# A hybrid attention and HGRN2 layer: the next input block prepared in mid-turn in the first head, eight shared buffers, half the descriptor area

## The chip, the cores and the metric

The kernel runs on one core of a Trainium2 chip. The metric is device time in microseconds (us), lower is better. TensorE is called PE, VectorE DVE, ScalarE ACT, GpSimd POOL and SyncE SP, as in the profile.

## What is computed

One layer over a sequence of 2048 rows of width 1024, all in float32:

```python
h = rmsnorm(x, ln1_w); proj = h @ w_in                 # 1024 -> 3584 columns
# four heads of differential attention (blocks of 128 queries, chunk-causal mask)
p = softmax(mask(q k^T / 8));  a = p[0] - lam * p[1];  o = rmsnorm(a @ v)
# four heads of HGRN2: a gated linear recurrence in chunks of 64 rows, with a carried state
x = x + concat(o_diff, o_hgrn) @ w_out
# feed-forward: up projection, causal convolution of width 3, SiLU gate, down projection
x = x + (silu(conv(u)) * v) @ w_down
```

## The kernel before

The program has four stages: the mixer (0 to about 1200 us), the output projection, the up projection and the down projection. The change is in the mixer, and one setting of it acts on the down projection too.

The mixer runs four heads one after the other (`s` = 0 to 3). A head does one attention head and one HGRN2 head over eight blocks of 256 rows (`b` = 0 to 7, called turns here). Each turn runs steps named by letters, in the order of a string:

```python
for b in range(NB):
    for c_ in ORDER if s else O0:
        nb_ = b + 1 + (c_ == "g" and s < GA) if c_ in "gABtuIJC" else b
        if nb_ < NB:
            step[c_](nb_)
```

The letters are: `g` makes or loads the normalized, transposed input block `hT`; `A`, `B` project q, k, v of the two halves of a block (24 matmuls of 384 columns each, L258 to L260); `I`, `J` project the value and gate of HGRN2 (24 matmuls of 256 columns each); `C` projects its query and forget gate (48 matmuls, tile `pjc`); `t`, `u` normalize and transpose q and k (tile `tpq`) and store `qT`; `a`, `b` are scores, maximum and exponentials of the two query blocks of a turn (tiles `sc`, `nm`, `p`); `x`, `y` blend the two softmaxes, transpose the blend and multiply with v (tiles `tpa`, `aT`, `av`); `h` is the level-by-level HGRN2 product (tiles `lt`, `kp`), `k` its output and state (tiles `op`, `sp`, `st`). `A`, `B`, `t`, `u`, `I`, `J`, `C` work on block b + 1, one turn ahead. In the first head `g` is one further ahead: in turn b it prepares block b + 2, so turns 0 to 5 hold it and turns 6 and 7 don't.

In the first head `g` is `phase1`: it loads two tiles `xt` of 128 rows (L225), squares and sums each on ACT (L233), takes the root on POOL (L103, L105), scales into `ht` on DVE (L235), transposes 16 blocks on PE into four PSUM tiles `tpx` (L241), evicts each in two halves by ACT (L244) and DVE (L245) into `hT`, and stores `hT` to DRAM (L247). In heads 1 to 3 `g` only loads `hT` back.

The order in which instructions reach each engine comes from the tile framework's list scheduler: the earlier an instruction stands in the program, the higher its priority; an instruction of lower priority goes ahead of one that isn't ready by the scheduler's own estimate. Engines then run their queues in order.

Buffers matter here. One pool, `pb`, with the tag `"p"` and `PBB` buffers of 4 KB a partition, holds the `xt` and `ht` of `phase1` (four of them for one block), the exponentials `p` of `a`, `b`, `x` and `y` (two for one query block in turns 0 to 3, four in turns 4 to 7, where the keys take two segments), and half of the first weight loads. In PSUM, `pj`, `pjc`, `tpq` and `tpx` share one tag with two buffers (`PJB`), and the scores `sc` have one (`SCB`).

The down projection keeps its sums in DRAM by 48 accumulating transfers that POOL issues (L830, `x2d<-acc`). Their descriptors are written by POOL into the area whose size `dynamic_dma_scratch_size` sets; all other transfers are issued by SP.

Of the kernel before, what the change touches and what calls it, by code (L numbers as in the profile page):

```python
# [67 lines left out]
def hymba_kernel(ctx, tc, x, ln1_w, w_in, q_norm_w, k_norm_w, lam_q1, lam_k1, lam_q2, lam_k2,  # L68
# [119 lines left out]
    with ExitStack() as ms:  # L188
# [73 lines left out]
        for s in range(4):  # L262
# [263 lines left out]
# [3 lines that stand above are left out]
# [353 lines left out]


ORDER = "gaABIbthJuxCyk"
O0 = "aABIbthJuxCgyk"
OF = "A1B23ItJuCg"
GA = 1
RB, QTB, FB, IGB, ATB, KVB, PBB = 4, 3, 2, 4, 3, 5, 6
SCB, PJB, MB = 1, 2, 2
AVT, AVB = "av", 1  # L890
HT, HB = "h", 1
# [35 lines left out]
```

## Time and profile before

| what | value |
|---|---|
| median of 3 runs | 2755.39 us (2753.69 to 2761.97) |
| the profiled execution, its own time | 2755.53 us |
| span of its trace | 2753.7 us |
| mean granted TensorE clock | 0.990 |
| PE busy / PEld (weight loads) busy | 2641.4 us (96%) / 2298.5 us (83%) |
| DVE, ACT, POOL busy | 1897.0 (69%), 1263.0 (46%), 1051.1 (38%) |

The span is the time from the first to the last instruction. A busy PE is a modelled figure: matmuls are pipelined, and one that starts while the one before still drains counts once.

### The profile page before, as it was taken

The numbers are of one execution on the slowest core, as the hardware profiler recorded it, in microseconds if no ns is written. First come the engines' busy times: TensorE is split into PE (matmuls) and PEld (weight loads), VectorE is DVE, ScalarE is ACT, GpSimd is POOL, SyncE is SP. The second block draws the span as 40 slices with busy tenths as digits, with TensorE's granted clock in tenths as the row PEclk, the third lists the DMA queues.
The fourth block names the chain that finished last, engine by engine and source line by source line (L and its number), as shares of the span: only waits on it lengthen the run. The fifth ranks groups of instructions, "written<-read, shape, count | busy, mean of one in ns | idle before, by whom it ended". The sixth has DMA issues, their size and how long they took to land. (4 is left out here: it accounts for less than half of the span.)

```text
span 2753.7 us, 42698 instructions
## 1 busy us (share of the span) xinstructions
PE 2641.4 (96%) x14722; PEld 2298.5 (83%) x14722; DVE 1897.0 (69%) x4058; ACT 1263.0 (46%) x3095; POOL 1051.1 (38%) x1168
## 2 busy tenths in 40 slices
PE   7999999999999999989999999999999998899999
PEld 6888999989999999978877888887888886687887
DVE  4677856676667666782337666668777769978787
ACT  4555644464446545553434434345434434334332
POOL 3222222212222222221234343443344346877775
PEclk9999999999999999999999999999999999999999
DMA  5333422232222322125754232235222224775754
GB/s 184 116 112 104 141 86 87 82 126 87 94 85 76 116 91 84 51 95 178 255 179 139 77 92 78 84 100 168 82 80 92 70 92 130 170 159 134 172 173 171
DMA packets 273492, 322.92 MB, mean 117 GB/s; under 512 B 19470, under 2 KB 238974, under 8 KB 269182
## 3 DMA queue, kind: packets, MB, share of 16 engines
q1 hardware_dynamic: 266366, 295.04, 32.7%
q0 software_dynamic: 6912, 25.17, 5.4%
q8 instruction: 117, 1.92, 0.3%
q14 instruction: 97, 0.79, 0.1%
HBM read 198.50 MB, written 104.86 MB: 110 GB/s over the span
## 5 line engine op out<-in xcount | busy, mean ns | idle before, releaser
L698 PE MATMUL q<-xT,WS 128*128 128x512 f32 x704 | 275.1, 391 | 2.3 <-DVE xT L631 2.2
L697 PE MATMUL q<-xT,WS 128*128 128x512 f32 x704 | 274.8, 390 | 2.3 <-ACT xT L630 2.3
L699 PE MATMUL q<-xT,WS 128*128 128x512 f32 x704 | 274.7, 390 | 0.0
L811 PE MATMUL pd<-TW,SG 128*128 128x512 f32 x616 | 245.0, 398 | 19.6 <-DVE acc L817 7.0
L813 PE MATMUL pd<-TW,SG 128*128 128x512 f32 x616 | 243.0, 396 | 3.3 <-DVE SG L631 3.3
L812 PE MATMUL pd<-TW,SG 128*128 128x512 f32 x616 | 244.0, 396 | 0.9 <-DVE TW L631 0.6
L630 ACT CAST WS<-st 128x512 fp32r<-128x512 f32 x176 | 108.5, 618 | 245.3 <-PE q L699 230.3
L698 PE MATMUL q<-xB,WS 128*128 128x512 f32 x528 | 207.1, 392 | 1.8 <-DVE xB L631 1.8
L697 PE MATMUL q<-xB,WS 128*128 128x512 f32 x528 | 207.3, 393 | 1.3 <-ACT xB L630 1.2
L699 PE MATMUL q<-xB,WS 128*128 128x512 f32 x528 | 206.9, 392 | 0.9 <-DVE WS L631 0.9
L387 ACT ACTIVATE p<-sc,nm 128x1024 f32<-128x1024 f32 (+4 forms) x192 | 165.5, 862 | 73.1 <-DVE nm L376 71.8
L631 POOL TENSOR_TENSOR WS<-st,WS 128x512 fp32r<-128x512 f32 x44 | 88.5, 2011 | 281.8 <-ACT WS L630 268.1
L376 DVE TENSOR_REDUCE nm<-sc 128x1 f32<-128x1024 f32 (+4 forms) x192 | 174.0, 906 | 12.6 <-PE sc L369 10.7
L258 PE MATMUL pj<-WA,hT 128*128 128x384 f32 x512 | 177.6, 347 | 2.6 <-DVE hT L245 2.6
L260 PE MATMUL pj<-WA,hT 128*128 128x384 f32 x512 | 175.4, 343 | 0.0
L259 PE MATMUL pj<-WA,hT 128*128 128x384 f32 x512 | 175.2, 342 | 0.0
L811 PEld LDWEIGHTS pd<-TW,SG 128*128 128x128 f32 x616 | 117.7, 191 | 49.9 <-DVE acc L817 8.3
L698 PEld LDWEIGHTS q<-xT,WS 128*128 128x128 f32 x704 | 132.5, 188 | 31.0 <-DVE xT L631 3.6
L697 PEld LDWEIGHTS q<-xT,WS 128*128 128x128 f32 x704 | 132.5, 188 | 30.0 <-ACT xT L630 2.8
L630 ACT CAST WS<-rawu 128x512 fp32r<-128x512 f32 x132 | 82.2, 624 | 163.4 <-PE q L699 163.0
L425 PE MATMUL av<-vst,aT 128*128 128x128 f32 x1088 | 151.0, 281 | 5.0 <-ACT aT L422 4.6
L699 PEld LDWEIGHTS q<-xT,WS 128*128 128x128 f32 x704 | 132.5, 188 | 27.4
(415 smaller groups left out, 7881.2 us busy)
## 6 DMA issues: line engine op xcount, KB each, us to landing
hT<-hTd SPq DMA_DIRECT2D x24, 2048.0 KB, 7.7
rawu<-in_w_up_dram SPq DMA_DIRECT2D x176, 256.0 KB, 3.0
x2d<-acc POOLq DMA_DIRECT2D x48, 512.0 KB, 6.4
gd<-c SPq DMA_DIRECT2D x176, 128.0 KB, 1.9
G<-gd SPq DMA_DIRECT2D x24, 768.0 KB, 4.4
hTd<-hT SPq DMA_DIRECT2D x8, 2048.0 KB, 6.2
qT<-qh SPq DMA_DIRECT2D x256, 64.0 KB, 2.0
rawd<-in_w_down_dram SPq DMA_DIRECT2D x22, 512.0 KB, 4.4
```

The lines of the kernel that those rows point to most:

```text
L258: PE.matmul(dst, lhsT=lh, rhs=rh, start=dt == 0, stop=False)
L259: PE.matmul(dst, lhsT=lh, rhs=rl, start=False, stop=False)
L260: PE.matmul(dst, lhsT=ll, rhs=rh, start=False, stop=dt == ND - 1)
L376: DVE.tensor_reduce(out=nm, in_=sc[:, 0:w], axis=AX.X, op=ALU.max, negate=True)
L387: ACT.activation(out=p[:, 0:w], in_=sc[:, 0:w], func=AF.Exp, bias=nm, accum_out=l)
L630: ACT.copy(dst[:, 0], src)
L697: PE.matmul(dst, lhsT=w[:, 0, cs], rhs=b_[:, 0, dt], start=dt == 0, stop=False)
L698: PE.matmul(dst, lhsT=w[:, 0, cs], rhs=b_[:, 1, dt], start=False, stop=False)
L699: PE.matmul(dst, lhsT=w[:, 1, cs], rhs=b_[:, 0, dt], start=False, stop=dt == 3)
L811: PE.matmul(pd, lhsT=Sx[n][:, 0, k], rhs=w[:, 0], start=k == 0, stop=False)
L812: PE.matmul(pd, lhsT=Sx[n][:, 0, k], rhs=w[:, 1], start=False, stop=False)
L813: PE.matmul(pd, lhsT=Sx[n][:, 1, k], rhs=w[:, 0], start=False, stop=k == len(qs) - 1)
```

## The change

In the first head the letter `g` moves from between `C` and `y` to between `I` and `b`. The pool `pb` gets eight buffers in place of six, in all four heads. The descriptor area shrinks from 8192 to 4096 bytes. Nothing else changes: no instruction is added or taken out.

```diff
 ORDER = "gaABIbthJuxCyk"
-O0 = "aABIbthJuxCgyk"
+O0 = "aABIgbthJuxCyk"
 OF = "A1B23ItJuCg"
 GA = 1
-RB, QTB, FB, IGB, ATB, KVB, PBB = 4, 3, 2, 4, 3, 5, 6
+RB, QTB, FB, IGB, ATB, KVB, PBB = 4, 3, 2, 4, 3, 5, 8
...
-    nc = bacc.Bacc("TRN2", target_bir_lowering=False, num_devices=1, dynamic_dma_scratch_size=8192)
+    nc = bacc.Bacc("TRN2", target_bir_lowering=False, num_devices=1, dynamic_dma_scratch_size=4096)
```

## Rows read from the trace of the kernel before

**Rows 1.** Busy time by stretch: six turns of the first head, the same of the second.

```profile
core 0: us, PE busy (x) PEld busy (x) DVE busy (x) ACT busy (x) POOL busy (x), PEclk, DMA share, GB/s
64.15:297.00 232.85, 215.78 (x1517) 201.40 (x1516) 160.99 (x535) 134.96 (x404) 58.66 (x119) 0.99 0.31 112
380.55:585.30 204.75, 200.79 (x1424) 187.78 (x1423) 135.79 (x484) 103.89 (x335) 48.45 (x95) 1.00 0.26 86
```

**Rows 2.** PE's waits from 64.15 to 297 us: total us, times, longest.

```profile
PE sc L368 <- ACT p L387: 5.5, 4, 2.3
PE tpx L241 <- DVE ht L235: 5.3, 5, 2.0
PE tpx L241 <- DVE hT L245: 2.6, 4, 0.9
```

**Rows 3.** Timeline of PE at the end of turn 5: start, us, instruction, wait.

```profile
273.47 0.33 PE L241 MATMUL tpx<-ident,ht 128*128 128x128 f32 x1 [1.98 <-DVE ht L235]
...
277.19 0.60 PE L241 MATMUL tpx<-ident,ht 128*128 128x128 f32 x4
277.63 0.39 PE L425 MATMUL av<-vst,aT 128*128 128x128 f32 x2
```

**Rows 4.** Timeline of SP: the loads of x in turns 1 and 5.

```profile
102.25 1.03 SPq L225 DMA_DIRECT2D xt<-in_xm_dram  x2
...
266.44 1.28 SPq L225 DMA_DIRECT2D xt<-in_xm_dram  x2
```

**Rows 5.** Timeline of ACT: last exponential of turn 1, first square of turn 5.

```profile
102.03 0.69 ACT L387 ACTIVATE p<-sc,nm 128x512 f32<-128x512 f32 x1 [0.55 <-DVE nm L376]
...
270.56 1.06 ACT L233 ACTIVATE ht<-xt 128x1024 f32<-128x1024 f32 x1 [3.96 <-DMA xt<-in_xm_dram]
```

**Rows 6.** The instructions of `phase1` by tile: ns min/median/max, first and last start.

```profile
L233 ACT ACTIVATE ht<-xt x16: 1049/1057/1062, 5.0 to 272.2; 128x1024 f32<-128x1024 f32 x16
L235 DVE TENSOR_SCALAR ht<-xt,r_r x16: 747/753/755, 9.8 to 274.3; 128x1024 f32<-128x1024 f32 x16
L244 ACT ACTIVATE hT<-tpx,ln1c x64: 453/473/508, 12.2 to 283.2; 128x256 fp32r<-128x256 f32 x64
L245 DVE SCALAR_TENSOR_TENSOR hT<-tpx,ln1c,hT x64: 474/478/485, 13.7 to 283.7; 128x256 fp32r<-128x256 f32 x64
```

**Rows 7.** Sums over six turns: projections `A`, `B`; the middle; the turn's end.

```profile
sum 53.80, PE 53.80 PEld 53.80 DVE 22.26 ACT 15.03 POOL 20.06; mean PE 8.97 PEld 8.97 DVE 3.71 ACT 2.51 POOL 3.34
...
sum 91.80, PE 90.78 PEld 84.79 DVE 74.00 ACT 56.26 POOL 21.62; mean PE 15.13 PEld 14.13 DVE 12.33 ACT 9.38 POOL 3.60
...
sum 93.80, PE 77.74 PEld 69.58 DVE 64.55 ACT 62.94 POOL 19.12; mean PE 12.96 PEld 11.60 DVE 10.76 ACT 10.49 POOL 3.19
```

**Rows 8.** Busy time by stretch, columns as in group 1: two stretches of half clock.

```profile
84.24:87.65 3.41, 3.41 (x14) 3.41 (x15) 2.31 (x8) 1.69 (x8) 0.42 (x2) 0.50 0.18 67
227.60:231.01 3.41, 3.41 (x15) 3.12 (x15) 1.97 (x7) 2.06 (x8) 0.74 (x2) 0.50 0.00 0
```

**Rows 9.** Timeline of PE in turn 6 of the second head.

```profile
596.16 0.60 PE L420 MATMUL tpa<-ident,p 128*128 128x128 f32 x4
597.84 0.50 PE L368 MATMUL sc<-kst,qT 128*128 128x512 f32 x1 [1.07 <-ACT p L387]
```

**Rows 10.** Timeline of ACT beside it: the third exponential of `b`.

```profile
596.81 0.88 ACT L387 ACTIVATE p<-sc,nm 128x768 f32<-128x768 f32 x1
```

**Rows 11.** PE's waits from 318 to 1190 us, the line on scores.

```profile
PE sc L368 <- ACT p L387: 1.7, 4, 1.1
```

**Rows 12.** The page's costliest groups: the maximum over the scores (mean ns last).

```profile
L376 DVE TENSOR_REDUCE nm<-sc 128x1 f32<-128x1024 f32 (+4 forms) x192 | 174.0, 906 | 12.6 <-PE sc L369 10.7
```

**Rows 13.** The page's DMA parts: POOL's queue, and its accumulating transfers (us to landing).

```profile
q0 software_dynamic: 6912, 25.17, 5.4%
...
x2d<-acc POOLq DMA_DIRECT2D x48, 512.0 KB, 6.4
```

**Rows 14.** Busy time while POOL issues them, columns as in group 1.

```profile
2318.00:2650.00 332.00, 316.57 (x1353) 256.79 (x1354) 274.95 (x347) 130.24 (x272) 262.44 (x223) 0.98 0.67 154
```

## The prediction

> **What bounds it.** I read the page first: PE is busy 96% of the span, so a change that adds and removes no instruction can only give back PE's idle time, or take more of it. The change reorders the first head, so I next compared equal pieces of two heads in the view of busy time by stretch. I cut both between the first transposes of q in turn 0 and in turn 6; the six turns between hold the same projections, attention and HGRN2 in either head, and the first head has `phase1` six times on top. The reader should compare lengths before shares: 232.85 us against 204.75, so the first head pays 28.1 us more [rows 1]. Of this, the transposes are real PE work: four take 0.44 us from start to start of what follows [rows 3], 0.11 each, and six blocks of 16 make 96 x 0.11 = 10.6 us. PE's idle time in the two pieces is 232.85 - 215.78 = 17.1 and 204.75 - 200.79 = 4.0 us, so 13.1 us more [rows 1]. The rest is clock: two stretches of 3.41 us ran at 0.50, that is at 1.2 instead of 2.4 GHz, each behind such a gap, and each loses half, 3.4 us together [rows 8]. 13.1 + 3.4 = 16.5 us is what better order could give back here (28.1 - 10.6 = 17.5 says the same by another way; I take the smaller).
>
> Where it sits is read from the sums over three kinds of stretches per turn. While `A` and `B` run, PE has no gap at all and DVE is busy 22.3 of 53.8 us. In the middle, from `I` to the last matmul of `C`, PE is busy 90.8 of 91.8. At the turn's end it is 77.7 of 93.8: 16.1 us, nearly all of the loss [rows 7]. The list of PE's waits names the cause: `tpx` for `ht` 5.3 us, `tpx` for the eviction of an earlier one 2.6 us, `sc` for an exponential 5.5 us [rows 2]. The timeline shows the first of these: PE has run out of `C` and stands 1.98 us before the first `tpx` [rows 3], because its data started late. The loads of x in a turn are issued just behind the last exponential of `b`: 102.25 us in turn 1 against 102.03 for that exponential [rows 4, 5]. In turn 5 they go out at 266.44, and ACT stands 3.96 us for them until the first square at 270.56 [rows 4, 5]. So `phase1` is a serial chain (load, square, root, scale, transpose, evict) that begins when the projections that could cover it are nearly used up.
>
> **The change, part by part.** The letter `g` ahead of `b` lets the loads follow the last exponential of `a` instead of that of `b`. In this trace `a` is done in the turn before or while `A` starts, so I expect them earlier by at least the 53.8 / 6 = 9 us that `A` and `B` take in a turn [rows 7]. Everything that the step issues moves with it: per turn two loads and one store of `hT` on SP, now ahead of the `qT` stores of `t` and `u`; two squares on ACT, 2 x 1.06 us; two small steps of the root per tile on POOL; two scalings on DVE, 2 x 0.75; 16 transposes on PE; and eight half evictions on each of ACT and DVE, 8 x 0.47 = 3.8 and 8 x 0.48 = 3.8 us [rows 6]. Squares and scalings cost nothing under `A` and `B`, where DVE has 53.8 - 22.3 = 31.5 us free over six turns and ACT 38.8 [rows 7]; if that cover failed they would be late by 2.1 + 1.5 us a turn, which is what PE waits for now. The stores on SP that now stand behind the loads feed only the next turn's scores.
>
> The evictions are the part with a price. They fall into the middle, where DVE is busy 74.0 of 91.8 us; with 6 x 3.8 = 22.9 more it is 96.9, against 91.8 + 10.6 = 102.4 us of PE work with the transposes in it, 95% [rows 6, 7]. The four `tpx` tiles now take turns with `I`, `J`, `t`, `u` and `C` for two PSUM buffers, so an eviction may hold up a projection. Below, this costs nothing, if other matmuls always cover it. Above, every one of four evictions a turn is exposed for its last pair, 0.47 + 0.48 = 0.95 us: 6 x 4 x 0.95 = 22.8 us. The nearest row is the 2.6 us that PE waits for these evictions now, with little beside them to run [rows 2]. I take one exposed eviction a turn, 5.7 us. At the end of the turn what is left looks like the second head's turn, whose 4.0 us of idle is already taken off.
>
> Eight buffers do two things. In the first head they are what lets `g` stand there: `a` holds two or four, `xt` and `ht` four, `b` two or four. In turns 4 and 5 `a` and `g` fill all eight, and `b` waits for the scalings and transposes; with `I`, `J` and `C` to run, I cost that at nothing beyond the evictions above. In all heads from turn 4 on they free the third and fourth exponentials of `b`, which with six must wait until the blend of `x` is transposed: those four transposes start at 596.16 us, the exponential at 596.81, and PE then stood 1.07 us before the next scores [rows 9, 10]. In the three later heads together PE waits only 1.7 us for exponentials [rows 11]. That is the upper bound of the gain, nothing the lower if order stays; I take half, 0.9 us.
>
> The descriptor area acts only on POOL's 48 transfers, of 6912 / 48 = 144 packets each, nine for each of 16 DMA engines [rows 13]. The trace shows no wait for space in the area, so half of it costs nothing unless it becomes too small; the upper bound stands with the rivals. The Trainium skill, DMA: Bandwidth & Descriptors (Terms; SWDGE vs HWDGE vs iDMA), says that a descriptor has 16 bytes and that POOL writes them into rings in a carved-out part of SBUF. By that, an estimate from the page's figure, 4096 bytes hold 256 descriptors on a partition, over twenty transfers of nine or ten, and the term is nothing; no run here shows the ring itself.
>
> The sum: 16.5 - 5.7 + 0.9 = 11.7 us. The profiled execution took 2755.53 us (span 2753.7), a tenth above the median of 2755.39, so no correction: 2755.5 - 11.7 = **2743.8 us**.
>
> **The rivals.** First, the stall only moves: two PSUM buffers and a DVE at 95% in the middle make PE wait for evictions there instead of at the end. For it speaks that `tpx` already waits for evictions [rows 2] and that the middle has little DVE time to spare [rows 7]; against it, that 72 long matmuls of `J` and `C` stand there and that work of DVE can slip to the turn's end, where `A` and `B` of the next block are now ready to cover it. Fully exposed it gives 16.5 - 22.8 = -6.3, so 2755.5 + 6.3 = 2761.8; between the two, at 8.2 to 22.8 us of exposure, the time stays within 2747.2 and 2761.8. The Trainium skill, Perfetto Trace Analysis (Optimization Strategy), says that a gap which repeats on the busiest engine can mean too few SBUF or PSUM tiles. By that rule the repeated wait would need a third `pj` buffer, which the change does not give, and the outcome would be this rival's; the trace agrees only for the 2.6 us, the other gaps come from late data.
>
> Second, the order doesn't change as it says: the loads still come late, since SP or a buffer holds them, or the scheduler places `tpx` behind `C` anyway. Then nothing moves, 2755. The issue time of the loads speaks for a tie to the buffers handed out in program order, so I hold this unlikely.
>
> Third, slower: eight buffers let scores run ahead. From turn 4 on, in all four heads, DVE would take two more maxima of 0.91 us [rows 12] before the blend of `x`, whose transposes and products then come when `C` is used up. 16 turns x 2 x 0.91 = 29.1 us if PE has nothing else; the gain of the first head is spent at 10.8 / 16 = 0.7 us a turn, and the full price gives 2755.5 - 10.8 + 29.1 = 2773.8. Against it: PE has up to 48 matmuls of `C` to run there, and idles only 4.0 us over six turns [rows 1].
>
> Fourth, the area is too small and POOL waits for one transfer of each pair to land: 24 x 6.4 = 154 us on an engine that is busy 262 of 332 us there [rows 13, 14], so up to 262 + 154 - 332 = 84 us, about 2828.
>
> **Chances.** A measurement of this kernel tells about 0.3% from no change, 8.3 us: faster means below 2747.2, slower above 2763.7. The forecast (8.3 to 18.2 us back, the last if no eviction shows and all 1.7 us come: 2737.3 to 2747.2) gets 0.60. The moved stall gets 0.23 and no change 0.07, both within 0.3%, 2747.2 to 2761.8. The scores ahead get 0.08 and the small area 0.02, above 2763.7. That is faster 0.60, same 0.30, slower 0.10. For eight in ten the range runs from 2736 to 2757: it leaves out the last two rivals and the worse half of a moved stall.
>
> **What would show it.** Right: loads of x issued under `A` in turns 0 to 5, ahead of the exponentials of `b`; no wait of `tpx` for `ht`; the six turns of the first head in about 222 us, with under 8 us idle and one or no stretch at half clock; heads 2 to 4 within 2 us of before. Wrong: waits of PE for `hT` or `pj` buffers between `I` and `C` that add up to over 8 us; turn ends of the first head no shorter; longer turns 4 to 7 in the later heads; POOL's transfers spread out. What would upset the forecast most is a reorder of the later heads, since they hold three quarters of the mixer and I assume that they stand still.

## The result: 0.6% slower

The changed kernel takes 2774.89 us (median of six runs, 2771.36 to 2776.52); the kernel before took 2756.22 beside it. The ratio is 1.0064 (95% interval 1.0052 to 1.0075), 18.7 us slower, where 2743.8 was predicted and 2736 to 2757 given as the range. Below, "so many us over (under) before" always means: median minus the median of the kernel before on the same chip.

### The profile page after: what moved, and what is told of

It reads as the page before. It is cut to its first block, busy times and chain, and to the rows that moved or that the text cites. A ratio compares the mean times of both kernels' runs of the same rounds, so it can differ in the third digit from the quotient of the medians.

```text
span 2774.1 us, 42674 instructions
## 1 busy us (share of the span) xinstructions
PE 2648.9 (95%) x14722; PEld 2302.0 (83%) x14722; DVE 1900.6 (69%) x4058; ACT 1263.8 (46%) x3095; POOL 1052.1 (38%) x1168
## 5 line engine op out<-in xcount | busy, mean ns | idle before, releaser
L376 DVE TENSOR_REDUCE nm<-sc 128x1 f32<-128x1024 f32 (+4 forms) x192 | 174.0, 906 | 14.9 <-PE sc L369 13.1
L258 PE MATMUL pj<-WB,hT 128*128 128x256 f32 x512 | 150.0, 293 | 7.6 <-DVE hT L245 5.2
```

Source lines behind the costliest of these rows:

```text
L258: PE.matmul(dst, lhsT=lh, rhs=rh, start=dt == 0, stop=False)
L376: DVE.tensor_reduce(out=nm, in_=sc[:, 0:w], axis=AX.X, op=ALU.max, negate=True)
```

## The profile after

The page of the changed kernel, its first lines:

```profile
span 2774.1 us, 42674 instructions
...
PE 2648.9 (95%) x14722; PEld 2302.0 (83%) x14722; DVE 1900.6 (69%) x4058; ACT 1263.8 (46%) x3095; POOL 1052.1 (38%) x1168
```

The span is 20.4 us longer with the same instructions. Busy time by stretch says where. First the changed kernel, with the same cuts (first q transposes of turn 0 and turn 6) as [rows 1]; turn 0's `g` now stands ahead of the cut, so its first row holds five `g` where [rows 1] held six, and its length is not to be set against 232.85. Then, for that comparison, the changed kernel from 60 us, when the first projections of block 1 run in both kernels, to the first q transposes of the second head:

```profile
70.98:313.23 242.25, 218.05 (x1490) 201.82 (x1490) 156.65 (x518) 129.07 (x385) 54.52 (x112) 0.96 0.29 103
398.85:604.05 205.20, 200.79 (x1424) 187.66 (x1423) 135.85 (x484) 103.98 (x335) 48.59 (x95) 1.00 0.26 86
60.00:398.85 338.85, 308.10 (x2135) 285.51 (x2135) 223.64 (x716) 181.37 (x534) 76.46 (x155) 0.97 0.30 102
```

The kernel before, from 60 us to the same transposes:

```profile
60.00:380.55 320.55, 300.12 (x2132) 281.38 (x2130) 222.15 (x717) 183.27 (x538) 79.21 (x156) 0.99 0.32 111
```

The second head is as it was, 205.20 us against 204.75 [rows 1]. The first head holds the loss: 338.85 - 320.55 = 18.3 us. PE's idle time grew from 320.55 - 300.12 = 20.4 to 338.85 - 308.10 = 30.8 us, so by 10.3, and nearly the same matmuls (2135 and 2132) were busy for 8.0 us longer. Most of these 8.0 are clock: five stretches of the six turns ran at 0.50 (1.2 GHz), where the kernel before had two [rows 8]; three more of 3.41 us lose 5.1; the other 2.9 I didn't trace. Two of the five, by stretch:

```profile
100.10:103.50 3.40, 3.40 (x16) 2.95 (x15) 2.60 (x7) 2.61 (x7) 0.00 (x0) 0.51 0.00 0
...
178.70:182.10 3.40, 3.39 (x13) 3.10 (x14) 1.39 (x5) 1.31 (x3) 0.46 (x1) 0.51 0.00 0
```

PE's longest waits in the six turns (total us, times, longest):

```profile
PE tpx L241 <- DVE ht L235: 9.0, 6, 3.4
PE pj L258 <- DVE hT L245: 5.2, 4, 2.1
PE tpq L305 <- DVE hT L245: 2.4, 3, 1.2
```

The first stood at 5.3 before; the other two are not among the rows of before [rows 2]. The wait of `sc` for exponentials, 5.5 us there, is down to one of 1.0 in the stretch from 60 to 330 us. One turn shows how the new ones come about. SP's timeline, the loads of x in turns 1 and 5, and in turn 1 the stores that stand just ahead of them:

```profile
86.09 0.32 SPq L499 DMA_DIRECT2D od<-o  x1
86.46 0.42 SPq L225 DMA_DIRECT2D xt<-in_xm_dram  x1
89.84 0.32 SPq L499 DMA_DIRECT2D od<-o  x1
90.25 0.39 SPq L225 DMA_DIRECT2D xt<-in_xm_dram  x1
...
255.13 0.90 SPq L225 DMA_DIRECT2D xt<-in_xm_dram  x2
```

They are earlier than before, 86.46 where 102.25 stood and 255.13 for 266.44 [rows 4]. In turn 1 each goes out right behind a store `od<-o` of the turn before, whose data `o` DVE has just written (85.71 to 86.06 for the first). But the root comes no earlier than the middle of the turn. POOL's timeline:

```profile
95.68 0.20 POOL L103 TENSOR_SCALAR rq_m<-ssq 128x4 f32<-128x4 f32 x1 [1.28 <-DVE ssq L294]
95.96 1.02 POOL L105 TENSOR_TENSOR rq_r<-rq_m,mhalf 128x4 f32<-128x4 f32 x1
97.05 0.61 POOL L296 TENSOR_TENSOR qn<-qr,rq_r 128x256 f32<-128x256 f32 x1
97.75 0.19 POOL L103 TENSOR_SCALAR r_m<-ss 128x1 f32<-128x1 f32 x1
98.02 0.55 POOL L105 TENSOR_TENSOR r_r<-r_m,mhalf 128x1 f32<-128x1 f32 x1
```

DVE's timeline, the two scalings, what stands between them, and the last eviction:

```profile
94.43 0.75 DVE L235 TENSOR_SCALAR ht<-xt,r_r 128x1024 f32<-128x1024 f32 x1 [3.02 <-POOL r_r L105]
95.17 0.42 DVE L294 TENSOR_REDUCE ssq<-qn 128x4 f32<-128x256 f32 x1
98.61 0.75 DVE L235 TENSOR_SCALAR ht<-xt,r_r 128x1024 f32<-128x1024 f32 x1 [3.02 <-POOL r_r L105]
...
107.15 0.48 DVE L245 SCALAR_TENSOR_TENSOR hT<-tpx,ln1c,hT 128x256 fp32r<-128x256 f32 x1
```

And PE's timeline:

```profile
99.42 1.10 PE L241 MATMUL tpx<-ident,ht 128*128 128x128 f32 x7 [2.25 <-DVE ht L235]
...
107.78 0.36 PE L258 MATMUL pj<-WB,hT 128*128 128x256 f32 x1 [1.44 <-DVE hT L245]
```

And ACT's, where the square of the second tile stands:

```profile
94.28 0.37 ACT L289 COPY qr<-pj 128x256 f32<-128x256 f32 x1 [2.29 <-PE pj L260]
...
94.71 0.43 ACT L292 ACTIVATE qn<-qr 128x256 f32<-128x256 f32 x1
95.03 1.06 ACT L233 ACTIVATE ht<-xt 128x1024 f32<-128x1024 f32 x1
95.97 0.20 ACT L233 ACTIVATION_READ_ACCUMULATOR ht<-xt 128x1 f32 x1
```

Read the four together. The new place puts squares, roots and scalings among the q/k normalization of `A` and `B`, and two in-order queues make the second `ht` late. On ACT its square stands behind the copy `qr` and the square `qn` of `B`, which wait for `B`'s last matmul; its sum is there at 96.17. On POOL the root `r_r` then stands behind `rq_m`, `rq_r` and `qn`, which need `B`'s sum `ssq`, and starts with `r_m` at 97.75, 1.58 us after its own sum was there. From the end of `ssq` at 95.59 to `ht` at 98.61 are just the 3.02 us that DVE stands. (On DVE `ssq` stands behind the first `ht`, which ends at 95.18, but its input `qn` is only done at 95.14: that order costs next to nothing here.) `A`, `B` and `I` are done by then, and PE waits 2.25 us for the transposes, with the clock at half behind it. The last of the four `tpx` tiles is evicted at 107.15 to 107.63. `J` needs the next of the two `pj` buffers, so its 24 matmuls, which need nothing of `phase1`, start only at 107.78.

## The experiments

### Which part of the change

Order alone, and buffers with area alone:

```diff
# e1_order_only: PBB 6, area 8192 as before
-O0 = "aABIbthJuxCgyk"
+O0 = "aABIgbthJuxCyk"
# e2_buffers_only: O0 as before
-RB, QTB, FB, IGB, ATB, KVB, PBB = 4, 3, 2, 4, 3, 5, 6
+RB, QTB, FB, IGB, ATB, KVB, PBB = 4, 3, 2, 4, 3, 5, 8
-    nc = bacc.Bacc("TRN2", target_bir_lowering=False, num_devices=1, dynamic_dma_scratch_size=8192)
+    nc = bacc.Bacc("TRN2", target_bir_lowering=False, num_devices=1, dynamic_dma_scratch_size=4096)
```

> Only the letter moves; six buffers and 8192 bytes stay. Theory: the order alone costs the time, since PE now waits for the prepared block between I and C instead of at the turn's end; 2771 to 2777 us, as with the whole change. Rival: the eight buffers cost it (scores that run ahead of the blend in all heads); then 2755 to 2759, as before.

> Eight buffers and 4096 bytes, the letter at its old place. Theory: nothing on any queue depends on them, 2754 to 2759 us. Rivals: scores run ahead in turns 4 to 7 of every head, or POOL waits for room for descriptors; then 2768 us or more.

Order alone took 2769.45 us, 16.3 over before (ratio 1.0058, 1.0037 to 1.0078), a little under the range that was expected. Buffers and area alone took 2753.14 against 2753.12 (ratio 1.0000, 0.9990 to 1.0009). So the order is the cause, and the other two edits do nothing; the order of instructions on each engine is the same with six and with eight buffers. The wait that the prediction put down to the sixth buffer [rows 9, 10] is still there with eight. PE's timeline with buffers and area alone, same place:

```profile
595.74 0.60 PE L420 MATMUL tpa<-ident,p 128*128 128x128 f32 x4
597.86 0.50 PE L368 MATMUL sc<-kst,qT 128*128 128x512 f32 x1 [1.52 <-ACT p L387]
```

### The PSUM buffers, at the new place

```diff
-                tp = pa.tile([P, 2, BLK], F32, name="tpx", tag="pj", bufs=PJB)
+                tp = ps.tile([P, 2, BLK], F32, name="tpx", tag="m", bufs=MB)
```

The tag `m` has two buffers, which only `tpa` uses otherwise. They are called own buffers below, though `tpa` shares them.

> The changed kernel, with the four tpx tiles in the two PSUM buffers of the blend's transposes (tpa) instead of the two of the projections. Theory, part one (the projections of J wait for the eviction of tpx): the 5.2 + 2.4 us that PE waits there for hT go, and half clock behind them, so 2760 to 2768 us. Rival (all of it is the late root on POOL, the 9.0 us that tpx waits for ht): 2771 us or more, and tpx still waits for ht.

2750.43 us, 2.7 under before (ratio 0.9988, 0.9978 to 0.9997), so 21.4 us come back, more than the 18.7 that were lost. PE's waits, from 60 to 330 us:

```profile
PE tpx L241 <- DVE ht L235: 8.6, 5, 3.6
PE tpq L305 <- ACT ig L327: 2.2, 4, 1.1
```

The waits of `pj` and `tpq` for evictions `hT` are gone, and the wait for `ht` is as long as ever. This alone would say that the buffers are the whole cause and the root costs nothing. The next group shows that this reading is wrong.

### The root

First the loads, squares, root and scalings as a step `G` of their own, ahead of `A` (`phase1` cut in two functions, `front` and `back`):

```diff
-O0 = "aABIgbthJuxCyk"
+O0 = "aGABIgbthJuxCyk"
```

> The changed kernel, with loads, squares, root and scaling of the block as a step of their own ahead of A, and only transposes and evictions at the new place. Theory, part two (the root stands on POOL's queue behind the q and k norm of A and B, and DVE stands 3.02 us for it): the 9.0 us that tpx waits for ht go, 2759 to 2768 us. Rival (the two PSUM buffers are all of it): 2771 us or more, with the waits of pj and tpq for hT as they are.

> The changed kernel with own PSUM buffers for tpx and the front half of phase 1 (loads, squares, root, scale) as a step of its own ahead of A. If the 8.6 us of tpx<-ht that stayed with the PSUM buffers alone can be had by an earlier start, 2740 to 2746; if the root stays behind the q/k norms in POOL's queue, as in the split without the PSUM buffers, 2748 to 2752.

With shared buffers 2772.07 us, 19.0 over before; with own buffers 2749.32, 4.0 under. The split changes neither by more than 1.3 us, and the root is no earlier by it: with shared buffers turn 1's first load goes out at 86.4 us, without the split at 86.5, and DVE stands 15.8 us for `r_r` between 80 and 180 us either way; with own buffers it stands 19.9 us from 60 to 330, without the split 20.0. SP's timeline shows what stands ahead of the loads: with the split and shared buffers, too, they go out right behind the two stores `od<-o` of the turn before (stores at 86.00 and 89.76, loads at 86.37 and 90.17). Whether they had found a free buffer earlier is not shown. So these two runs say nothing on what a late root costs. Leaving the root out of the scaling does; it is still computed, but `ht` no longer waits for it, and the output is not the layer's:

```diff
-                DVE.tensor_scalar(out=ht, in0=xt, scalar1=r, scalar2=None, op0=ALU.mult)
+                DVE.tensor_scalar(out=ht, in0=xt, scalar1=1.0, scalar2=None, op0=ALU.mult)
```

> The changed kernel with phase 1's scale by the root replaced by a scale of 1.0, so that ht no longer waits for POOL (the output is not the reference's; the root itself is still computed). If the late root on POOL is what costs (rival theory R), the wait tpx<-ht of 9.0 us goes and the time falls to 2753 to 2762. If the PSUM buffers cost (theory A), it stays above 2766, with pj<-hT and tpq<-hT still there.

2758.36 us, 5.0 over before (ratio 1.0012, 1.0003 to 1.0022): 13.7 of the 18.7 us come back with the buffers still shared. PE's waits, from 60 to 330 us:

```profile
PE tpq L305 <- DVE hT L245: 3.0, 3, 1.8
PE pj L258 <- DVE hT L245: 2.9, 2, 1.5
...
PE tpx L241 <- DVE ht L235: 1.5, 2, 1.1
```

Both theories had claimed most of the loss, and each got it. My next theory was that they are one chain (late root, late `tpx`, late eviction, `J` blocked), which is mended by cutting either link; then both cuts together give little more than one.

> Both links of the chain cut at the new place: own PSUM buffers for tpx, and a scale of 1.0 in place of the root (the output is not the reference's). If the late root and the shared buffers are one chain, of which cutting either link gives back nearly all, the two cuts together give little more than the better one: 2744 to 2750. If they were two costs of their own (16.5 and 24 us), they would add up to 2734 or less.

2737.27 us, 16.4 under before. The two cuts give 21.4 and 13.7 alone and 35.1 together, which is their sum, though each figure is good only to some 3 to 5 us. The one-chain theory falls: at the new place the shared buffers and the late root are two costs.

Since a scale of 1.0 also changes what the list scheduler reckons with, the real root was tried earlier, with `G` as the first step of the turn:

```diff
-O0 = "aGABIgbthJuxCyk"
+O0 = "GaABIgbthJuxCyk"
```

> The changed kernel with own PSUM buffers and the front half of phase 1 as the first step of the turn, ahead of a. If the root can be brought ahead of the q/k norms on POOL in this way, the waits tpx<-ht (8.6 us) go and it comes to the kernel without the root, 2737 to 2742. If the loads still come too late for the middle of the same turn, 2747 to 2751, as with the front half ahead of A.

> The changed kernel, transposes in pj's buffers as before, with the front half of phase 1 as the first step of the turn. If the lateness of ht is what the shared buffers turn into 16.5 us, this comes to the kernel with the root left out, 2754 to 2762. If leaving the root out helped by taking work away, or in the list scheduler's order only, it stays above 2766.

With own buffers 2738.52 us, 15.5 under before (without the root: 16.4 under); with shared ones 2761.87, 7.2 over (without the root: 5.0 over). The second is only just inside the 2754 to 2762 that were expected; both agree with the kernels without the root within 2.2 us. In the first, the loads go out at 73.98 and 79.06 us, no wait of `tpx` for `ht` is left, and POOL's timeline has the first root ahead of the q/k normalization:

```profile
82.23 0.22 POOL L103 TENSOR_SCALAR r_m<-ss 128x1 f32<-128x1 f32 x1 [0.21 <-ACT ht L239]
82.53 0.55 POOL L105 TENSOR_TENSOR r_r<-r_m,mhalf 128x1 f32<-128x1 f32 x1
84.28 0.19 POOL L103 TENSOR_SCALAR rq_m<-ssq 128x4 f32<-128x4 f32 x1 [1.20 <-DVE ssq L305]
```

So it is the lateness of `ht` that costs, not the work of the root; loads and squares came earlier here along with the root.

### What the old place already paid

The same two cuts, and the same split, with `g` behind `C` as before:

> The kernel before with the four transposes' PSUM tiles tpx taken out of the two buffers of pj and put into the two of the blend's transposes (g at its old place, eight buffers, the small area). If sharing pj's two buffers costs only in the middle of a turn, where J follows (theory A), this stays at the kernel before, 2750 to 2756 us, and the 2.7 us by which the same edit at the new place beats the kernel before is what the new order is worth. If the share costs at either place (theory B), this too gets faster, by 3 us or more, and the new order is worth nothing by itself.

> The kernel before with phase 1's scale by the root replaced by a scale of 1.0 (the output is not the reference's). At the new place this gave back 16.5 us. If the root stands late on POOL only at the new place, the time stays at 2750 to 2754; if it was as late at the old one, it falls by 10 or more, to 2743 or less. The trace of before has tpx<-ht at 5.3 us there, so a fall of 3 to 8, 2745 to 2750, is likeliest.

> The kernel before with own PSUM buffers for tpx and a scale of 1.0 (the output is not the reference's): neither cost, at the old place. If the two costs are all that the new place is worse by, this equals the same pair at the new place, 2737.3 within 4 us. If the old place is better by itself, it is under 2733; if the new one is, over 2742.

Over (+) or under (-) before, in us, each column a way to treat the two costs:

| place of `g` | shared, root | shared, no root | own, root | own, no root |
|---|---|---|---|---|
| behind `C` (old) | 0 | +1.1 | -9.1 | -13.8 |
| ahead of `b` (new) | +18.7 | +5.0 | -2.7 | -16.4 |
| new minus old | +18.7 | +3.9 | +6.4 | -2.6 |

The old place paid for shared buffers too, 9.1 us: theory B of the run with own buffers at the old place holds. [rows 2] name 2.6 us of waits for them, but that stretch leaves out the start of the kernel, where PE waits for evictions of the first blocks. PE's timeline before:

```profile
16.25 1.94 PE L241 MATMUL tpx<-ident,ht 128*128 128x128 f32 x8 [3.47 <-DVE hT L245]
20.58 0.66 PE L258 MATMUL pj<-WA,hT 128*128 128x384 f32 x1 [2.39 <-DVE hT L245]
```

With own buffers at the old place the first projection starts 8 us earlier:

```profile
12.61 0.69 PE L258 MATMUL pj<-WA,hT 128*128 128x384 f32 x1
```

PE's waits for `hT` from 0 to 330 us add up to 8.7 us before, close to the 9.1. At the new place the start gains as well: the projections of block 1 start at 46.17 us with own buffers and at 51.69 with shared ones, so some 5.5 of the 21.4 us lie there. The last row of the table is a difference of places and is free of it.

The late root cost nothing that was measured at the old place with shared buffers (the expected fall of 3 to 8 us didn't come) and 4.7 us with own ones. Leaving it out doesn't make `ht` early there: with own buffers PE still waits 5.9 us for it from 60 to 330 us, as ACT's squares stand 12.9 us for the loads. With neither cost the new place comes out 2.6 us better, but the intervals of the two kernels overlap (0.9923 to 0.9956 and 0.9932 to 0.9965), and with the front half first the old place is ahead (below): what the place is worth by itself isn't shown. By the table the loss of 18.7 us is -2.6 for the place, 13.7 - 4.7 = 9.0 for the root, (5.0 + 16.4) - (1.1 + 13.8) = 6.5 for the buffers, and 18.7 + 2.6 - 9.0 - 6.5 = 5.8 by which the two costs overlapped at the old place (14.9 and 4.7 apart, 13.8 together) and no longer do at the new one. With intervals of 2.6 to 4.5 us to either side for the entries this split is rough, and -2.6 and 5.8 aren't clear of noise.

> The kernel before with the loads, squares, root and scale of phase 1 as a step ahead of A, the transposes in pj's buffers at the old place. With own buffers the split gave 7.5 us and took away every wait tpx<-ht. If the two edits are apart, 2744 to 2748 here; if the shared buffers hide it, 2751 to 2755.

> The kernel before with own PSUM buffers for tpx and the front half of phase 1 as a step of its own ahead of A, while the transposes stay at their old place. If the 8.8 us of tpx<-ht that the same kernel without the split still shows can be had by an earlier start of the loads, squares and roots, 2734 to 2740 us. If not, 2743 to 2747.

> Own buffers, transposes at the old place, the front half as the first step of the turn. With the front half ahead of A the kernel took 2736.7 and had no wait tpx<-ht left, so nothing more is to be had by a still earlier start: 2734 to 2740. If the earlier loads take buffers from the exponentials of a, it is slower, 2741 or more.

The front half ahead of `A` (`aGABIbthJuxCgyk`) with shared buffers took 2749.13 us, 4.9 under before (ratio 0.9979, 0.9970 to 0.9988), which is between the two answers that were expected. With own buffers it took 2736.73, 16.9 under (ratio 0.9938, 0.9923 to 0.9953), and as the first step of the turn 2736.25, 18.4 under (0.9938, 0.9920 to 0.9956): the same, no more is to be had that way. Both beat the kernel before and the changed one. Busy time of the second of them in the cut of [rows 1], where 232.85 us stood:

```profile
61.09:275.07 213.98, 210.78 (x1512) 196.35 (x1511) 157.56 (x525) 132.09 (x398) 57.95 (x117) 1.00 0.33 117
```

PE's waits of the first of the two, from 60 to 330 us, all of one us or more:

```profile
PE lt L465 <- DVE qP L471: 3.7, 7, 1.2
PE sp L499 <- ACT op L507: 1.5, 2, 0.8
PE sc L379 <- ACT p L398: 1.2, 1, 1.2
PE lt L465 <- DVE sc L383: 1.0, 1, 1.0
```

Nothing of `phase1` is in the list any more.

### Other places

Is it the place by itself, with `C` last and alone?

```diff
-O0 = "aABIgbthJuxCyk"
+O0 = "aABIbthJguxCyk"     # e10 shared, e13 own buffers
+O0 = "aABIbthJuxgCyk"     # e12 own buffers
```

> The changed kernel with g one step later still, behind J instead of ahead of b; the transposes keep their place in pj's two buffers. If what costs is that J's projections (and with them C and the HGRN2 chain) stand behind the evictions of tpx in those buffers (theory A), most of the 20 us is gone: 2752 to 2760 us, with no wait pj<-hT. If any place ahead of C costs (theory B: C last and alone, with nothing left to fill beside it), it stays at 2765 to 2775.

> Own PSUM buffers for tpx with g between J and u, the place that took 2781.6 with shared buffers. If the shared buffers are what made that place the slowest of all (the transposes tpq and pjc standing behind the evictions of tpx), about 30 us of it go: 2745 to 2752. If the place itself costs, it stays above 2765.

> Own PSUM buffers for tpx with g between x and C, one step ahead of its old place. If the old place is best because block b + 2 then has the longest time to load, this is 1 to 3 us slower than with g behind C (2744.2); if any place behind J will do once the buffers are its own, 2742 to 2747.

Behind `J` with shared buffers is the slowest of all, 2781.59 us, 28.3 over before, and against my expectation: `J` no longer waits, but the transposes `tpq` of `u` now do. PE's waits, from 60 to 330 us:

```profile
PE tpq L305 <- DVE hT L245: 7.6, 6, 2.4
...
PE tpx L241 <- DVE hT L245: 3.1, 4, 1.3
```

With own buffers the same place takes 2757.57, 3.9 over before: 24.3 us of it were the buffers. The 13.0 us by which it is still behind the old place with own buffers I didn't trace to one wait; in the same stretch PE waits 6.3 us with `sp` for `op` and 3.4 with `av` for `oo`, where the old place has 0.5 and nothing. Just ahead of `C` with own buffers it is 2745.57, 8.1 under, 1.0 from the old place, no difference that was measured.

## Why the prediction was wrong

- **Where the time lies** was right. 16.5 us were said to be there to recover in the first head; the five kernels that cut both costs come to 13.8 to 18.4 us under before. In the prediction's own cut (q transposes of turn 0 to turn 6) the best of them, old place, own buffers and front half first, takes 213.98 us for 232.85, with 3.2 us of idle time and the clock at 1.00. That the totals lie so close to 16.5 is in part luck: 3.1 us of this kernel's lead (64.15 - 61.09) come ahead of the cut, from the start, which the prediction didn't count.
- **The loads come earlier** was right, by 11 to 16 us in the turns shown. The tie to the exponentials is not what the traces show: the exponential of [rows 5] ends at 102.72, after the loads of 102.25 went out, and these stand on SP right behind four stores `qT` (99.60 to 102.15). "No wait of `tpx` for `ht`" was wrong: 9.0 us in place of 5.3.
- **The step that failed first: what moves with `g` was costed at nothing under `A` and `B`.** Squares, root and scalings were held against DVE's and ACT's free time there [rows 7]. Free time wasn't the question; the order in the queues was. POOL's two small steps were counted and then given no queue. They stand behind the q/k normalization, and the second square stands behind `B`'s copies on ACT; each of the two waits of DVE for a root in the turn shown is 3.02 us. This term was 0 in the sum and is 13.7 us, 9.0 more than at the old place with own buffers.
- **The step that failed second: the exposed evictions, 5.7 us.** What the sharing of `pj` costs at the new place is 21.4 us. Less the 5.5 at the start, about 16 are left for the turns, an estimate from the two traces, between the 5.7 taken and the upper bound of 22.8 that the prediction left to a rival. I sized it by the row of 2.6 us of waits at the old place. At the new place `J` and the q/k transposes stand behind the same evictions: from 60 to 330 us PE waits 5.2 + 2.4 + 0.7 = 8.3 us for `hT`, and three more stretches ran at half clock than with own buffers (five and two), another 5.1 us.
- **The buffers, 0.9 us, and the area, 0:** measured 0.0 together. The mechanism for the 0.9 was wrong: the third exponential did not wait for a buffer, since the wait stands with eight. So was "eight buffers are what lets `g` stand there": order alone with six gave the same loss.
- **The rivals.** The moved stall was the right one in kind and had 0.23, but its bound of 2761.8 held evictions alone, on the ground that everything ahead of the transposes is covered. The Trainium skill, Perfetto Trace Analysis (Optimization Strategy), says that a gap which repeats on the engine that should be saturated can mean too little SBUF or PSUM for the next tile, the buffer count being one cause; the runs agree, with 21.4 us at the new place and 9.1 at the old for two buffers of another tag. Scores running ahead and the small area did not happen: the second head is 205.20 us against 204.75, and buffers and area alone take the time of before.

## What to carry to other kernels

When a step moves earlier, write down for each in-order queue which instructions it now stands between: here loads behind stores on SP, a square behind the copies of `B` on ACT, a root behind the q/k normalization on POOL. Such a chain can end late although every engine in it has free time. Before tiles of a moved step rotate through a shared pair of PSUM buffers, ask what independent work takes the next buffer of the pair, and give the step buffers of its own if any tag is less used. Two suspected causes are told apart by removing both: here either cut alone seemed to explain most of the loss, and only the pair showed that they add. And before a row of waits sizes a cost, check that its stretch holds all of it: the 2.6 us of [rows 2] left out 5.9 at the start.

## What was not expected of the hardware

A short gap of PE can cost more than itself: in the changed kernel PE stands 2.25 us until 99.42 and the clock is at 0.51 from 100.10 to 103.50 us, another 1.7 us; over the first head 10.3 us of added idle time went with 8.0 us of longer busy time for nearly the same matmuls. Not each gap did: in the kernel before PE stands 2.25 us until 238.58, and the granted clock from 238.60 to 242.00 is 1.00. And a place that looks free by busy shares was not: POOL is busy 54.52 of 242.25 us in these turns, 23%, and its queue, with ACT's, still set when the transposes could start.
